# A hybrid decoder layer in fp32: even pauses in all eight mixer units, a later sample update in unit 0, products column tile by column tile, and ragged ends transposed together

## The chip, the cores and the metric

One core of one Trainium2 chip runs the whole program. The metric is the device time of one execution in microseconds (us), taken as the median of three runs. A profiled execution of the same program gives the trace from which the durations below are read; its own time stands beside its span in the table. TensorE is called PE here, VectorE DVE, ScalarE ACT, GpSimd POOL, and the queue of SyncE, which issues the DMAs, SP.

## The reference

One layer over 280 tokens: 16 learned meta tokens, 256 prompt tokens and 8 sample tokens, each sample with recurrent states of its own. The width is 2048; all is fp32.

```python
def decoder_layer(x, pos, s_ret, s_hg, prompt, ...):
    x = layer_norm(ALPHA * x + 0.5 * swiglu(x, f1_g, f1_u, f1_d), ln1_g, ln1_b)
    m, s_ret, s_hg = token_mixer(x, pos, s_ret, s_hg, prompt, w_in, lb, hg_norm_g, w_out)
    x = layer_norm(ALPHA * x + m, ln2_g, ln2_b)
    x = layer_norm(ALPHA * x + 0.5 * swiglu(x, f2_g, f2_u, f2_d), ln3_g, ln3_b)

def token_mixer(...):      # x @ w_in is split into ten parts of 2048 columns
    q_r, k_r, v_r, g_r, q_h, f_h, i_h, g_h, a_r, a_h = jnp.split(x @ w_in, N_PROJ, axis=-1)
    ...                    # retention: 8 heads of 256; HGRN2: 16 heads of 128, k = 1 - f
    y = jax.nn.sigmoid(a_r) * o_r + jax.nn.sigmoid(a_h) * o_h
    return y @ w_out, s_ret, s_hg

def retention_chunk(S, q, k, v):
    inner = jnp.einsum('bhid,bhjd->bhij', q, k) * D
    o = jnp.einsum('bhij,bhjv->bhiv', inner, v) + jnp.einsum('bhid,bhdv->bhiv', q_dec, S)
    S_new = jnp.exp(lg * C)[:, None, None] * S + jnp.einsum('bhjd,bhjv->bhdv', k_dec, v)
```

HGRN2 has the same form with a decay of its own for each feature and token. For each sample token both mixers read a state from memory, decay it, add one outer product of key and value, read the output from it with the query, and write it back. The two kinds of state of the 8 samples come to 8 MB for HGRN2 and 16 MB for retention, read once and written once.

## The kernel before

Features lie on the 128 partitions, tokens on the free axis: 280 columns, or 264 where the meta tokens are dropped. A weight of the width 2048 has 16 chunks of 128 features. Each fp32 weight product is made as three faster products (`dense()`, the matmul on L217): the weight's upper part by the input's upper part, the upper by the input's lower part (`xl`), and the weight's lower part (`wlo`) by the input's upper part. The weights stream in blocks of eight 128x128 tiles, 512 KB each (`stream()`): SP loads `raw`, ACT casts the upper part `whi` (L187), DVE subtracts for the lower part `wlo` (L188). There are three buffers of each, so a block is asked for some two blocks ahead of its use.

The program has three stages: the first feed-forward half-step (to about 742 us of the span), the mixer (to about 1790 us), and the output product with the second half-step. The change lies in the mixer alone. The mixer works in 8 units, each with one head of retention and two heads of HGRN2. For each unit `project()` makes six products of two chunks each (f, q_h, i_h, q_r, k_r, v_r), and then the four gate products of the unit before (g_r with a_r, g_h with a_h, twice). A step is one k-chunk of such a product: two weight tiles, six matmuls, about 0.7 us. A group has 16 steps, a unit 160.

Between the steps run the mixers' own small matmuls and transposes. Two generators for each unit, `mix_hg(u)` and `mix_ret(u)`, are started when their inputs are ready; each `yield n` is a pause of n steps, and after each step `pump()` counts the pauses down and lets a thread issue its next piece. So the order on PE is written out by hand, by these pauses. The order on ACT, DVE, POOL and SP is made by a scheduler that follows the program's priorities and its own estimates; there an instruction waits behind all that stands ahead of it on its engine.

In `mix_hg` the scores of a unit come level by level: `blocks()` makes the masked levels with 32-column tiles of PE (`pl`), later levels (16, 32, 64 tokens) use K and Q scaled on DVE, and a pause separates them. `calm` is an extra pause of two steps; it was left out in units 1 and 7 of `mix_hg` and in unit 7 of `mix_ret`, while unit 1 had two steps more at some places (`2 * (u == 1)`). Then K is transposed (`ptk`), the states of the samples are updated (`smh`, on ACT and DVE), and state, sample outputs and outputs are made (`pst`, `pq`, `po`, `pv`).

In `mix_ret` v and k are transposed, 128 tokens at a time (`pt`), cast and scaled (`vs`, `ks`), then come the scores (`psc`), the state (`psr`, copied by ACT to `sro`), and the samples' update: ACT scales the four loaded states by gamma (L1073, `smr<-smr,gam` for the first four samples and `smr<-smr,sro` for the last four), DVE adds the outer products (L1078), with each sample's value row spread over the partitions by a DMA (`vbr<-vrd`). Outputs (`pqr`, `por`, `pvr`) follow. The tokens do not divide by 128: 24 of k's and v's 280 columns and 16 of K's 272 are ragged ends, with a transpose of their own for each chunk or head.

Of the kernel before, what the change touches and what calls it, by code (L numbers as in the profile page):

```python
# [10 lines left out]
F32 = mybir.dt.float32  # L11
# [3 lines left out]
ALU = mybir.AluOpType  # L15
# [3 lines left out]
P = 128  # L19
# [31 lines left out]

SCORES = ((0, 0, SEQ, P), (SEQ, P - NMETA, 2 * P - P + NMETA, P), (2 * SEQ - P + NMETA, SEQ - NMETA, NMETA, LP - 2 * P))
# [75 lines left out]
def trunk(ctx: ExitStack, tc: tile.TileContext, A, O):  # L128
# [417 lines left out]
    with tc.tile_pool(name="yp", bufs=1) as yp:  # L546
# [7 lines left out]
        with tc.tile_pool(name="mp", bufs=1) as mp:  # L554
# [33 lines left out]
            qdh = tmp("qdh", (P, 2, NS * 32))  # L588
            qdr = tmp("qdr", (P, 2, NS * 32))
            nc.gpsimd.memset(qdh, 0.0)  # L590
            nc.gpsimd.memset(qdr, 0.0)
            vsm = tmp("vsm", (P, P))
# [8 lines left out]
            sc2 = tmp("sc2", (P, NMETA), dt=F32R)  # L601
            for z in (km, vm, ks2, vs2, sc2):
                z = z if len(z.shape) == 2 else z.rearrange("p c f -> p (c f)")
                nc.scalar.copy(z, qdh[:, 0, : z.shape[1]])
# [106 lines left out]
            def upper_upper_lower(out, x):  # L711
                n = x.shape[0]
                nc.scalar.copy(out[:n], x)
                nc.scalar.copy(out[32 : 32 + n], x)
                sub(out[64 : 64 + n], x, out[:n].bitcast(F32))
# [7 lines left out]
            def alone(qd, q):  # L723
                for e in range(2):
                    nc.vector.tensor_copy(qd[:, :, 128 * e + e : 128 * e + 128 : 32], q[:, :, SEQ + 4 * e : SEQ + 4 * e + 4])

            def sample_columns(on, po, os):

                nc.tensor.transpose(po[:, 3 * P :], os, ident)
                nc.vector.tensor_copy(  # L730
                    on[:, SEQ:].rearrange("p (e j) -> p e j", e=2), po[:, 3 * P :].rearrange("p (j c) -> p c j", c=32)[:, 0:2, :])

            def mix_hg(u, f, k, q, v):

                calm = 2 if u != 1 and u < HR - 1 else 0
# [62 lines left out]
                def blocks(x, s, own=None):  # L798

                    x = x.rearrange("p i (x j c) -> p i x j c", x=4, j=4)  # L800
                    for h in range(2):
                        pl = mx_bank("pl")
                        half = pl[:, : 2 * 80].rearrange("p (b c) -> p b c", b=2)
                        for b in range(2):
                            for j in range(0, P, 32):
                                kk = K[:, h, NMETA + b * P + j : NMETA + b * P + j + 32]
                                o = half[j : j + 32, b, :48].rearrange("p (i c) -> p i c", i=3)
                                nc.tensor.matmul(o, kk, x[:, :, 2 * h + b, j // 32, :], start=True, stop=True, tile_position=(0, j))
                                if own is not None:
                                    nc.tensor.matmul(  # L810
                                        half[j : j + 32, b, 48:], kk, own[:, h, b * P + j : b * P + j + 32],
                                        start=True, stop=True, tile_position=(0, j))
# [42 lines left out]
                for s in (4, 8):  # L855
                    scale_k(s)
                scale_q(8)
                join(8)
                yield W_LEVEL + 4 + 2 * (u == 1) + calm
                for s in LEVELS[MASKED:]:  # L860
# [29 lines left out]
                    yield W_LEVEL + 2 * (u == 1) + calm  # L890
# [6 lines left out]
                for h in range(2):  # L897
# [3 lines left out]
                    for b, (t0, n) in enumerate(((NMETA, P), (NMETA + P, P), (0, NMETA))):  # L901
                        nc.tensor.transpose(pt[:n, b * P : (b + 1) * P], K[:, h, t0 : t0 + n], ident)
                    nc.scalar.copy(kt, pt[:, : 2 * P].rearrange("p (b f) -> p b f", b=2))
                    upper_upper_lower(km[:, h, :], pt[:NMETA, 2 * P : 3 * P])
# [27 lines left out]
                for h in range(2):  # L932
                    for b in range(NS):
                        j = 32 * (b % 4)
                        nc.tensor.matmul(
                            pq[j : j + 32, h * P : (h + 1) * P], qdh[:, h, 32 * b : 32 * b + 32], sms[h][:, b, :],
                            start=b < 4, stop=b >= 4, tile_position=(0, j))
                os = tmp("osh", (P, 2 * P))
                nc.scalar.copy(os, pq[:, : 2 * P])
                yield 4  # L940

                def outputs(h):
# [5 lines left out]
                    sample_columns(on[:, h, :], po, os[:, h * P : (h + 1) * P])  # L948
# [31 lines left out]
            def mix_ret(u, q, k, v):  # L980
# [3 lines left out]
                calm = 2 if u < HR - 1 else 0  # L984
# [11 lines left out]
                nc.sync.dma_start(dt, A["dtab"][u])  # L996
                for c in range(2):
                    pt = mx_bank("pt")
                    for b, (t0, n) in enumerate(BLOCKS):
                        nc.tensor.transpose(pt[:n, b * P : (b + 1) * P], v[:, c, t0 : t0 + n], ident)  # L1000
                    nc.scalar.copy(vt[:, :, c, :], pt[:, : 2 * P].rearrange("p (b f) -> p b f", b=2))
                    nc.scalar.copy(vt2[:NB, c, :], pt[:NB, 2 * P : 3 * P])
                    f = slice(c * P, (c + 1) * P)
                    split(vs[:, 0, :, f], vs[:, 1, :, f], vt[:, :, c, :])
                    upper_lower_upper(vs2[:, c, :], vt2[:NB, c, :])
                    yield 1
                    pt = mx_bank("pt")
                    for b, (t0, n) in enumerate(BLOCKS):
                        nc.tensor.transpose(pt[:n, b * P : (b + 1) * P], k[:, c, t0 : t0 + n], ident)
                    for b, (t0, n) in enumerate(BLOCKS):  # L1010
                        x, g = pt[:n, b * P : (b + 1) * P], dec[:n, b, u : u + 1]
                        his = [ks[:, 0, b, f]] if b < 2 else [ks2[third[0], c, :], ks2[third[1], c, :]]
                        for hi in his:
                            nc.scalar.activation(hi, x, AF.Copy, scale=g)
                        nc.vector.scalar_tensor_tensor(
                            out=(ks[:, 1, b, f] if b < 2 else ks2[third[2], c, :]), in0=x, scalar=g,
                            in1=his[0].bitcast(F32), op0=ALU.mult, op1=ALU.subtract)
# [18 lines left out]
                gams = [tmp("gam", (P, 1))]  # L1036
                nc.gpsimd.tensor_scalar(
# [219 lines left out]
```

## Time and profile before

| what | value |
| --- | --- |
| median of 3 runs | 2599.12 us (2597.02 to 2599.78) |
| profiled execution, its own time | 2593.9 us |
| its span | 2592.1 us |
| PE busy | 2570.6 us, 99% of the span |
| DVE, ACT busy | 1703.8 us (66%), 1374.9 us (53%) |
| granted clock of PE | 0.999 |
| one steady unit (units 2 to 6) | 128.6 us |
| idle time of PE that ends on a wait | some 16 us in all |

A row of the timeline has the start in us from the span's start, the duration, the engine, the line, the operation, what is written and read by the program's names, and the number of such instructions; in square brackets stand the idle time of the engine just before it and what ended that. A matmul's shown duration is longer than the distance to the next, since they are pipelined: a cost on PE is read from the distance of starts. A row of the windows has, for each engine, its busy time in the stretch and the number of its instructions, then PE's granted clock, the share of time in which the DMA engines were busy, and GB/s.

### The profile page before, as it was taken

How to read it: one execution, taken by the hardware profiler on the slowest of the kernel's cores; microseconds unless marked ns; L12 is line 12 of the kernel's file. 1: busy time of each engine (PE TensorE's matmuls, PEld its weight loads, DVE VectorE, ACT ScalarE, POOL GpSimd, SP SyncE). 2: the span in 40 equal slices, each digit the busy share in tenths (PEclk: the TensorE clock that was granted, in tenths of full speed). 3: DMA queues.
4: the chain of work that ended last, by engine and by line, in shares of the span. 5: the costliest groups of instructions: out<-in, count | busy, mean ns of one | idle time of the engine just before them, and what ended most of it. 6: DMA issues, size and time to landing. Idle time of an engine off the chain costs nothing.

```text
span 2592.1 us, 56133 instructions
## 1 busy us (share of the span) xinstructions
PE 2570.6 (99%) x23400; PEld 2543.1 (98%) x23400; DVE 1703.8 (66%) x2859; ACT 1374.9 (53%) x2160; POOL 19.6 (1%) x78
## 2 busy tenths in 40 slices
PE   9999999999999999999999999999999999999999
PEld 9999999999999999999999999999999999999998
DVE  6544444565579787777787878786985555556555
ACT  5444444444456665757575757574564444444444
POOL 0000000000000000000000000000000000000000
PEclk9999999999999999999999999999999999999999
DMA  7555555555566786767676767666656666666664
GB/s 242 187 184 184 186 183 184 187 180 186 185 200 208 243 277 208 256 213 253 216 250 219 254 212 253 213 225 195 194 186 199 196 195 196 195 196 194 197 195 148
DMA packets 156895, 536.25 MB, mean 207 GB/s; under 512 B 17952, under 2 KB 25952, under 8 KB 156640
## 3 DMA queue, kind: packets, MB, share of 16 engines
q1 hardware_dynamic: 156352, 532.37, 63.2%
q8 instruction: 183, 3.00, 0.5%
q14 instruction: 72, 0.59, 0.1%
q10 hardware_dynamic: 288, 0.29, 0.0%
HBM read 501.99 MB, written 30.61 MB: 205 GB/s over the span
## 4 chain that ended last, share of the span: by engine, by line
PE 59%; DVE 1%; ACT 1%; issue 0%; POOL 0%; DVEq 0%; ACTq 0%; POOLq 0%
PE up L217 17%; PE dn L217 9%; PE wo L217 3%; PE pj_g_r L217 3%; PE pj_g_h L217 3%; PE pj_a_h L217 3%; PE pj_k_r L217 3%; PE pj_a_r L217 3%; PE pj_v_r L217 3%; PE pj_q_r L217 2%; PE pj_i_h L217 2%; PE pj_f L217 2%; PE pj_q_h L217 2%; DVE wlo L188 0%; PE pqr L1091 0%; PE por L1106 0%
## 5 line engine op out<-in xcount | busy, mean ns | idle before, releaser
L188 DVE TENSOR_TENSOR wlo<-raw,whi 128x1024 fp32r<-128x1024 f32 (+1 forms) x869 | 1062.8, 1223 | 762.1 <-ACT whi L187 760.5
L187 ACT CAST whi<-raw 128x1024 fp32r<-128x1024 f32 (+1 forms) x870 | 905.6, 1042 | 938.1 <-PE up L217 419.2
L217 PE MATMUL up<-xh,whi 128*128 128x280 f32 (+1 forms) x2624 | 725.6, 280 | 0.8 <-ACT whi L187 0.8
L217 PE MATMUL up<-xh,wlo 128*128 128x280 f32 (+1 forms) x2624 | 725.8, 280 | 0.4 <-DVE wlo L188 0.4
L217 PE MATMUL up<-xl,whi 128*128 128x280 f32 (+1 forms) x2624 | 725.4, 279 | 0.0
L217 PEld LDWEIGHTS up<-xh,whi 128*128 128x128 f32 x2624 | 492.6, 189 | 1.0 <-ACT whi L187 1.0
L217 PEld LDWEIGHTS up<-xh,wlo 128*128 128x128 f32 x2624 | 492.6, 189 | 1.0 <-DVE wlo L188 1.0
L217 PEld LDWEIGHTS up<-xl,whi 128*128 128x128 f32 x2624 | 492.6, 189 | 0.0
L217 PE MATMUL dn<-hh,whi 128*128 128x280 f32 (+1 forms) x1376 | 384.7, 280 | 0.0
L217 PE MATMUL dn<-hl,whi 128*128 128x280 f32 (+1 forms) x1376 | 384.3, 279 | 0.0
L217 PE MATMUL dn<-hh,wlo 128*128 128x280 f32 (+1 forms) x1376 | 384.3, 279 | 0.0
L217 PEld LDWEIGHTS dn<-hh,whi 128*128 128x128 f32 x1376 | 260.1, 189 | 0.1
L217 PEld LDWEIGHTS dn<-hl,whi 128*128 128x128 f32 x1376 | 260.1, 189 | 0.1
L217 PEld LDWEIGHTS dn<-hh,wlo 128*128 128x128 f32 x1376 | 260.1, 189 | 0.0
L217 PE MATMUL pj_g_r<-xh,whi 128*128 128x264 f32 x256 | 76.8, 300 | 0.0
L217 PE MATMUL pj_k_r<-xh,whi 128*128 128x280 f32 x256 | 73.7, 288 | 0.0
L217 PE MATMUL pj_g_h<-xh,whi 128*128 128x264 f32 x256 | 73.6, 288 | 0.0
L217 PE MATMUL pj_v_r<-xh,whi 128*128 128x280 f32 x256 | 73.5, 287 | 0.0
L217 PE MATMUL pj_v_r<-xh,wlo 128*128 128x280 f32 x256 | 72.4, 283 | 0.3 <-DVE wlo L188 0.3
L217 PE MATMUL pj_k_r<-xh,wlo 128*128 128x280 f32 x256 | 72.4, 283 | 0.0
L217 PE MATMUL pj_v_r<-xl,whi 128*128 128x280 f32 x256 | 72.3, 283 | 0.0
L217 PE MATMUL pj_k_r<-xl,whi 128*128 128x280 f32 x256 | 72.3, 283 | 0.0
(396 smaller groups left out, 5230.3 us busy)
## 6 DMA issues: line engine op xcount, KB each, us to landing
raw<-in_w_up SPq DMA_DIRECT2D x343, 512.0 KB
raw<-in_w_in SPq DMA_DIRECT2D x320, 512.0 KB
raw<-in_w_dn SPq DMA_DIRECT2D x172, 512.0 KB
smr<-in_sr SPq DMA_DIRECT2D x32, 512.0 KB
out_srs<-smr SPq DMA_DIRECT2D x32, 512.0 KB
raw<-in_w_out SPq DMA_DIRECT2D x32, 512.0 KB
smh<-in_sg SPq DMA_DIRECT2D x16, 512.0 KB
vbr<-vrd SPq DMA_DIRECT2D x32, 256.0 KB
```

Source lines behind the costliest of these rows:

```text
L187: nc.scalar.copy(hi[:, j:jn, :], raw[:, j:jn, :])
L188: nc.vector.tensor_tensor(out=lo[:, j0:j1, :], in0=raw[:, j0:j1, :], in1=hi[:, j0:j1, :].bitcast(F32), op=ALU.subtract)
L217: nc.tensor.matmul(o, w, t, start=start, stop=stop)
```

## The change

- `calm` is 2 in every unit of both mixers, and the special pauses of unit 1 are gone. Units 1 and 7 get the spacing of units 2 to 6.
- In unit 0 the pause behind the second state copy of retention is 10 steps rather than 2: the update of the samples' states, and the load of the last four samples' states (`load(1)`), come eight steps later.
- `blocks()` issues for each 128 tokens first the four 48-column products, one for each column tile, and then the four 32-column products, where before both products of a column tile stood next to each other.
- Ragged ends: POOL gathers the last 24 columns of both chunks of k and v in one tile (`tails`), which is transposed once in a unit rather than four times; POOL gathers the first 16 columns of both heads' K (`meta`), one transpose rather than two. The sample outputs of both HGRN2 heads are summed into one result of 128 columns (the queries are laid out with a row length of 129, `ALONE`, so that a head's queries take columns of their own), one copy and one transpose rather than a double-width copy and two transposes. The casts of v's ragged rows are made for both chunks at once and stand ahead of k's.
- `gam`, the tile with gamma, is made by POOL from the copy of the first half of retention's state, where before it was made from the scores. ACT's scaling of the first four samples therefore comes behind that copy. For the last four samples DVE takes the keys from a small copy that POOL makes (`late_k`).

```diff
-                calm = 2 if u != 1 and u < HR - 1 else 0          # mix_hg
+                calm = 2
...
-                            for j in range(0, P, 32):
-                                kk = K[:, h, NMETA + b * P + j : NMETA + b * P + j + 32]
-                                o = half[j : j + 32, b, :48].rearrange("p (i c) -> p i c", i=3)
-                                nc.tensor.matmul(o, kk, x[:, :, 2 * h + b, j // 32, :], start=True, stop=True, tile_position=(0, j))
-                                if own is not None:
+                            for mine in range(1 if own is None else 2):
+                                for j in range(0, P, 32):
+                                    at = b * P + j
+                                    o, y = half[j : j + 32, b, :48].rearrange("p (i c) -> p i c", i=3), x[:, :, 2 * h + b, j // 32, :]
+                                    if mine:
+                                        o, y = half[j : j + 32, b, 48:], own[:, h, at : at + 32]
                                     nc.tensor.matmul(
-                                        half[j : j + 32, b, 48:], kk, own[:, h, b * P + j : b * P + j + 32],
-                                        start=True, stop=True, tile_position=(0, j))
+                                        o, K[:, h, NMETA + at : NMETA + at + 32], y, start=True, stop=True, tile_position=(0, j))
...
+                nc.gpsimd.tensor_copy(meta[:, :, :NMETA], K[:, :, :NMETA])
...
-                yield W_LEVEL + 4 + 2 * (u == 1) + calm
+                yield W_LEVEL + 4 + calm
...
-                    yield W_LEVEL + 2 * (u == 1) + calm
+                    yield W_LEVEL + calm
...
-                    for b, (t0, n) in enumerate(((NMETA, P), (NMETA + P, P), (0, NMETA))):
-                        nc.tensor.transpose(pt[:n, b * P : (b + 1) * P], K[:, h, t0 : t0 + n], ident)
+                    for b in range(2):
+                        t0 = NMETA + b * P
+                        nc.tensor.transpose(pt[:, b * P : (b + 1) * P], K[:, h, t0 : t0 + P], ident)
+                    x = pt[:64, 2 * P : 3 * P]
+                    if h == 0:
+                        nc.tensor.transpose(x, meta.rearrange("p h t -> p (h t)"), ident)
...
-                calm = 2 if u < HR - 1 else 0                     # mix_ret
+                calm = 2
...
+                for i, x in enumerate((k, v)):
+                    nc.gpsimd.tensor_copy(tails[:, 2 * i : 2 * i + 2, :NB], x[:, :, 2 * P :])
                 for c in range(2):
                     pt = mx_bank("pt")
-                    for b, (t0, n) in enumerate(BLOCKS):
-                        nc.tensor.transpose(pt[:n, b * P : (b + 1) * P], v[:, c, t0 : t0 + n], ident)
+                    for b in range(2):
+                        nc.tensor.transpose(pt[:, b * P : (b + 1) * P], v[:, c, b * P : (b + 1) * P], ident)
...
-                    upper_lower_upper(vs2[:, c, :], vt2[:NB, c, :])
...
+                    if c == 0:
+                        nc.tensor.transpose(pt[:, 2 * P : 3 * P], tails.rearrange("p i t -> p (i t)"), ident)
+                    if c == 0:
+                        for i in range(2):
+                            r = 64 + 32 * i
+                            nc.scalar.copy(vt2[:NB, i, :], pt[r : r + NB, 2 * P : 3 * P])
+                        upper_lower_upper(vs2.rearrange("p c f -> p (c f)"), vt2.rearrange("p c f -> p (c f)")[:NB])
...
-                gams = [tmp("gam", (P, 1))]
-                nc.gpsimd.tensor_scalar(
-                    out=gams[0], in0=scr[:, 0:1], scalar1=GAMMA[u], scalar2=GAMMA[u], op0=ALU.min, op1=ALU.max)
...
-                    yield 2
+                    if c == 0:
+                        gams = [tmp("gam", (P, 1))]
+                        nc.gpsimd.tensor_scalar(
+                            out=gams[0], in0=so[:, 0:1], scalar1=GAMMA[u], scalar2=GAMMA[u], op0=ALU.min, op1=ALU.max)
+                    yield 2 if u or c == 0 else 10
                 load(1)
...
+                late_k = late[:, 1:].rearrange("p (c b) -> p c b", c=2)
+                nc.gpsimd.tensor_copy(late_k, k[:, :, LP + 4 :])
```

How the order moves, at three places. PE in unit 2, where the first chunk of v and k is transposed between the steps of a gate product, before:

```order
L1000 MATMUL pt<-ident,v 128x128 x2
L1000 MATMUL pt<-ident,v 24x128
L217 MATMUL pj_g_r_12858<-xh_3_9240,whi_12861 128x264
L217 MATMUL pj_g_r_12858<-xl_3_9241,whi_12861 128x264
L217 MATMUL pj_g_r_12858<-xh_3_9240,wlo_12862 128x264
L217 MATMUL pj_a_r_12859<-xh_3_9240,whi_12861 128x264
L217 MATMUL pj_a_r_12859<-xl_3_9241,whi_12861 128x264
L217 MATMUL pj_a_r_12859<-xh_3_9240,wlo_12862 128x264
L1009 MATMUL pt<-ident,k_r 128x128 x2
L1009 MATMUL pt<-ident,k_r 24x128
```

And the same place of PE now:

```order
L1022 MATMUL pt<-ident,v 128x128 x2
L218 MATMUL pj_g_r_12851<-xh_3_9247,whi_12854 128x264
L218 MATMUL pj_g_r_12851<-xl_3_9248,whi_12854 128x264
L218 MATMUL pj_g_r_12851<-xh_3_9247,wlo_12855 128x264
L218 MATMUL pj_a_r_12852<-xh_3_9247,whi_12854 128x264
L218 MATMUL pj_a_r_12852<-xl_3_9248,whi_12854 128x264
L218 MATMUL pj_a_r_12852<-xh_3_9247,wlo_12855 128x264
L1029 MATMUL pt<-ident,k_r 128x128 x2
L1031 MATMUL pt<-ident,tails 128x128
```

One transpose has gone from the first gap; the second has as many as before, and reads the new tile `tails`. In units 2 to 6 the gaps stand behind the same steps as before.

DVE in unit 0, around the retention samples' update (`smr<-vbr,k_r,smr`), between the lower parts of blocks 30 to 32 of the mixer's weights (`wlo30` to `wlo32`), before; `vbr_9960` holds the first value rows of the last four samples:

```order
L239 TENSOR_TENSOR K_9490<-K_9490,T4_9683 128x68x4
L254 TENSOR_TENSOR vs2_8641<-vt2_8636,vs2_8641 24x256
L239 TENSOR_TENSOR K_9490<-K_9490,T8_9892 128x34x8
L1078 SCALAR_TENSOR_TENSOR smr_9701<-vbr_9813,k_r_9445,smr_9701 128x256
L188 TENSOR_TENSOR wlo30_10032<-raw30_10030,whi30_10031 128x8x128
L1078 SCALAR_TENSOR_TENSOR smr_9703<-vbr_9813,k_r_9445,smr_9703 128x256 x2
L239 TENSOR_TENSOR T2_10876<-f_9916 128x272
L239 TENSOR_TENSOR T4_11042<-T2_10876 128x136
L239 TENSOR_TENSOR T8_11170<-T4_11042 128x68
L188 TENSOR_TENSOR wlo31_10091<-raw31_10089,whi31_10090 128x8x128
L1078 SCALAR_TENSOR_TENSOR smr_9937<-vbr_9960,k_r_9445,smr_9937 128x256
L188 TENSOR_TENSOR wlo32_10128<-raw32_10126,whi32_10127 128x8x128
```

And the same stretch of DVE now:

```order
L240 TENSOR_TENSOR K_9497<-K_9497,T8_9893 128x34x8
L1112 SCALAR_TENSOR_TENSOR smr_9707<-vbr_9810,k_r_9452,smr_9707 128x256
L189 TENSOR_TENSOR wlo30_9989<-raw30_9987,whi30_9988 128x8x128
L1112 SCALAR_TENSOR_TENSOR smr_9709<-vbr_9810,k_r_9452,smr_9709 128x256 x2
L1112 SCALAR_TENSOR_TENSOR smr_9707<-vbr_9812,k_r_9452,smr_9707 128x256 x2
L1112 SCALAR_TENSOR_TENSOR smr_9709<-vbr_9812,k_r_9452,smr_9709 128x256 x2
L189 TENSOR_TENSOR wlo31_10082<-raw31_10080,whi31_10081 128x8x128
L240 TENSOR_TENSOR T2_10875<-f_9918 128x272
L240 TENSOR_TENSOR T4_11053<-T2_10875 128x136
L240 TENSOR_TENSOR T8_11216<-T4_11053 128x68
L189 TENSOR_TENSOR wlo32_10131<-raw32_10129,whi32_10130 128x8x128
```

Six instructions of the update stood ahead of block 30's lower part before, two do now; six stand between blocks 30 and 31; and none on the last four samples stands ahead of block 32's any more. On SP the load of the second HGRN2 state (`smh`, 512 KB), which was issued behind the mixer's weight block 38, now stands between blocks 32 and 33, ahead of the two loads of the last four retention samples' states.

ACT in unit 2, between the last scaling of k and the second state copy, before:

```order
L880 COPY acch<-pl 64x2x64 x2
L1073 ACTIVATE smr<-smr,gam 128x1024
L187 CAST whi_13231<-raw_13230 128x8x128
L1073 ACTIVATE smr<-smr,gam 128x1024
L1058 COPY sro<-psr 128x256
L908 ACTIVATE smh<-smh,fs 128x128 x5
L1058 COPY sro<-psr 128x256
```

And now:

```order
L894 COPY acch<-pl 64x2x64 x2
L188 CAST whi_13219<-raw_13218 128x8x128
L927 ACTIVATE smh<-smh,fs 128x128 x3
L1084 COPY sro<-psr 128x256
L927 ACTIVATE smh<-smh,fs 128x128
L1106 ACTIVATE smr<-smr,gam 128x1024 x2
L1084 COPY sro<-psr 128x256
```

The two long scalings moved behind the first state copy, and the weight cast and three HGRN2 scalings moved ahead of them.

70 lines of the change are left out of this document (44 added, 26 removed).

## The prediction

> **What bounds the kernel.** I read the page's head first, then the stretch of one whole unit in the middle, then the rows of PE that carry a wait.
>
> ```profile
> span 2592.1 us, 56133 instructions
> PE 2570.6 (99%) x23400; PEld 2543.1 (98%) x23400; DVE 1703.8 (66%) x2859; ACT 1374.9 (53%) x2160; POOL 19.6 (1%) x78
> PEclk9999999999999999999999999999999999999999
> ```
>
> ```profile
> 1100.00:1228.60 128.60, 128.60 (x1274) 125.85 (x1273) 98.58 (x200) 82.45 (x156) 1.64 (x5) 1.00 0.71 235
> 1192.00:1200.00 8.00, 8.00 (x73) 7.90 (x72) 7.56 (x20) 7.96 (x18) 0.00 (x0) 1.00 0.95 330
> 836.00:844.00 8.00, 6.94 (x89) 6.58 (x88) 6.72 (x17) 5.05 (x6) 0.10 (x1) 1.00 0.90 310
> ```
>
> PE is the bound, at full clock: in a steady unit it is busy for all of 128.60 us, so a matmul taken away there shortens the span, as long as the weights keep up. The second row is the stretch in which they only just do (ACT busy 7.96 of 8 us). The third lies in unit 0, where PE does wait. The mixer's waits on PE:
>
> ```profile
> 840.01 0.38 PE L217 MATMUL pj_q_h<-xh,wlo 128*128 128x264 f32 x1 [1.06 <-DVE wlo L188]
> 847.51 0.39 PE L217 MATMUL pj_i_h<-xh,wlo 128*128 128x280 f32 x1 [1.31 <-DVE wlo L188]
> 852.09 0.41 PE L872 MATMUL pl<-Q,K 128*32 128x32 f32 x13 [2.40 <-DVE Q L239]
> 953.77 0.33 PE L902 MATMUL ptk<-ident,K 128*128 128x128 f32 x1 [1.45 <-DVE K L239]
> 969.09 0.30 PE L729 MATMUL por<-ident,osr 128*128 128x128 f32 x1 [1.75 <-ACT yh L224]
> 1692.16 0.33 PE L902 MATMUL ptk<-ident,K 128*128 128x128 f32 x1 [0.61 <-DVE km L254]
> 1701.72 0.38 PE L1056 MATMUL psr<-vs,ks 128*128 128x256 f32 x1 [1.48 <-DVE ks L1015]
> 1738.78 0.38 PE L236 MATMUL pvr<-rhi,ones_r 128*128 128x264 f32 x1 [0.37 <-ACT rhi L224]
> 1739.96 0.38 PE L236 MATMUL pvr<-rlo,ones_r 128*128 128x264 f32 x1 [0.81 <-DVE rlo L225]
> ```
>
> Three lie in unit 0 (4.77 us), two in unit 1 (3.20), four in unit 7 (3.27): just the units whose pauses are edited. Units 2 to 6 have none. So there are 11.2 us of waits to win, beside PE's own work.
>
> **Ragged ends.** Three transposes in a gap between dense products:
>
> ```profile
> 1172.52 0.28 PE L217 MATMUL pj_a_r<-xl,whi 128*128 128x264 f32 x1
> 1172.63 0.28 PE L217 MATMUL pj_a_r<-xh,wlo 128*128 128x264 f32 x1
> 1172.75 0.49 PE L1009 MATMUL pt<-ident,k_r 128*128 128x128 f32 x3
> 1172.99 0.36 PE L217 MATMUL pj_g_r<-xh,whi 128*128 128x264 f32 x1
> 1173.19 0.28 PE L217 MATMUL pj_g_r<-xl,whi 128*128 128x264 f32 x1
> ```
>
> A dense product starts 0.11 us after the one before it. From 1172.63 to 1173.19 pass 0.56 us, of which two dense products are 0.23; the three transposes cost 0.33, so 0.11 each. A unit loses five (two of v, one of k, one of K, one of the sample outputs; the first two and the next two become one and one): 40 x 0.11 = 4.4 us. The gathering copies on POOL are new, and this is how such copies run:
>
> ```profile
> 1134.22 0.97 POOL L737 COPY ends<-v 128x32 f32<-128x32 f32 x1 [75.17 <-ACT v L658]
> 1135.13 0.20 POOL L738 COPY ends<-v 128x32 f32<-128x32 f32 x1
> ```
>
> ```profile
> 1133.90 1.23 DVE L188 TENSOR_TENSOR wlo<-raw,whi 128x1024 fp32r<-128x1024 f32 x1 [1.42 <-ACT whi L187]
> ```
>
> ```profile
> 1170.28 0.40 ACT L675 COPY v<-pj_v_r 128x280 f32<-128x280 f32 x1
> ```
>
> The first copy took 0.97 us and ended at 1135.19, just behind the subtraction on DVE (1135.13); the next one took 0.20. In unit 2, v's second chunk is there at 1170.68 and the gap of k's first chunk is at 1172.75, 2.07 us later; a copy held behind a whole subtraction takes some 1.2 us, so the gathering of v lies hidden, with 0.9 us to spare, behind the gate products. I cost it at 0 (bounds: 0, and 1 us in each unit if one more subtraction comes between). `meta` is gathered over 20 steps before its use and has more cover. That POOL's reads hold up DVE I cost at 0 as well, since DVE is busy for 98.58 of 128.60 us in a unit; the bound is 4 reads x 8 units x 0.20 = 6.4 us. The copies that ACT and DVE save (two 24-row copies, two 24-row casts, the double-width sample copy) lie off the path and are worth nothing but slack.
>
> The Trainium skill (SBUF — State Buffer, "Who interferes with whom") says that a DVE instruction with two inputs in SBUF and a GpSimd instruction that reads SBUF take the same port by an exclusive lock, so that the second waits for the first to end. The copy above agrees (0.97 us behind the subtraction, 0.20 alone). By this rule each of the four added reads in a unit (two of `tails`, `meta`, the late keys) would also hold up DVE; if all of that fell on the path, the sum below would be -6.7 instead of -13.1.
>
> **Column tiles in turn.** The masked levels with and without the 32-column products:
>
> ```profile
> 1144.85 0.31 PE L808 MATMUL pl<-Qm,K 128*32 128x48 f32 x8
> 1145.69 0.39 PE L217 MATMUL pj_k_r<-xh,whi 128*128 128x280 f32 x1
> ...
> 1155.18 0.55 PE L808 MATMUL pl<-Qm,K 128*32 128x48 f32 x32
> 1155.66 0.39 PE L217 MATMUL pj_k_r<-xh,whi 128*128 128x280 f32 x1
> ```
>
> With them (64 products) the gap lasts 0.84 us, without (32) 0.48. So 32 products of 32 columns cost 0.36. The 32 of 48 columns, whose neighbours go to different column tiles, cost 0.48 less the 0.12 of a change-over, also 0.36. Taken in turn the narrower ones should cost 32/48 of that, 0.24: a gain of 0.12 in a unit, 1.0 us in eight. Bounds: 0 (the distance is set per instruction), and 8 x 0.36 = 2.9 (they vanish behind the others); I take 1.0, by the row of the same tiles.
>
> Against this speaks the Trainium skill (TensorE: Matmul & The Clock Gate, Part 3, "The mechanism"): a weight load overlaps running matmuls only where it goes to other rows of the array. All column tiles here use all 128 rows, so by that rule the order of the columns would change nothing, this term would be 0 and the sum -12.1. The cheap gap of 32 is as the column order lets one expect, but no row here has the other order with equal widths.
>
> **What of these 5.4 us is given back.** A steady unit has one tight place:
>
> ```profile
> 1325.48 0.28 PE L217 MATMUL pj_g_r<-xl,whi 128*128 128x264 f32 x1
> 1325.67 0.38 PE L217 MATMUL pj_g_r<-xh,wlo 128*128 128x264 f32 x1
> 1325.89 0.28 PE L217 MATMUL pj_a_r<-xh,whi 128*128 128x264 f32 x1
> ```
>
> Here a product comes 0.19 rather than 0.11 us after its neighbour, and the next 0.22 after it: the lower part was only just ready, behind ACT's fullest stretch (its like in unit 2 is the second windows row). PE will come there about 0.6 us earlier, while ACT has a few thin copies and casts less to do before it. I take 0.14 us a unit as given back in units 2 to 6, +0.7 us (bounds 0, and 5 x 0.68 = +3.4).
>
> **Pauses in units 1 and 7.** Unit 7 gets the spacing of units 2 to 6, which show no wait in any of their gaps: -3.27 us (bounds 0 and -3.27). Its last piece comes 18 steps later, still 10 steps ahead of the first gate product of unit 7 that could wait for it being done, so nothing is added at the end. In unit 1 the transposes of K come four steps (2.8 us) later, and the wait of 1.45 at 953.77 goes. The one at 969.09 stands behind a step that does not move, and waits for the sample outputs that DVE centres among many updates of HGRN2, which now come four steps later: I take half, -0.9 (bounds 0 and -1.75).
>
> **Unit 0's sample update, eight steps on.** DVE and ACT there:
>
> ```profile
> 834.71 1.27 DVE L1078 SCALAR_TENSOR_TENSOR smr<-vbr,k_r,smr 128x256 f32<-128x256 f32 x3
> ...
> 845.84 0.48 DVE L1078 SCALAR_TENSOR_TENSOR smr<-vbr,k_r,smr 128x256 f32<-128x256 f32 x1 [3.00 <-DMA vbr<-vrd]
> 846.24 1.22 DVE L188 TENSOR_TENSOR wlo<-raw,whi 128x1024 fp32r<-128x1024 f32 x1
> ...
> 851.62 0.42 DVE L239 TENSOR_TENSOR Q<-Q,T 128x256 f32<-128x256 f32 x1
> ```
>
> ```profile
> 840.72 1.15 ACT L1073 ACTIVATE smr<-smr,sro 128x1024 f32<-128x1024 f32 x1 [2.50 <-DMA smr<-in_sr]
> 842.29 1.15 ACT L1073 ACTIVATE smr<-smr,sro 128x1024 f32<-128x1024 f32 x1 [0.42 <-DMA smr<-in_sr]
> ```
>
> Four update instructions fewer stand ahead of block 30's lower part, 0.42 us each; but since they also wait less for their inputs I take only two of them as time saved, 0.85 of the wait of 1.06 at 840.01. The scaling of Q, which stood behind eight updates of the last four samples (from 845.84 on), now stands right behind block 32's lower part, some 3.5 us earlier: the 2.40 at 852.09 goes. Block 32 no longer waits behind DVE's 3.00 us for value rows. But its cast on ACT stands behind the scalings of the last four states, as before, and their loads now have 512 KB of HGRN2 state ahead of them: at 310 GB/s, 1.7 us. That brings the cast from 843.4 to some 845.1 and the lower part to 847.3, where it was 847.46 before. So the 1.31 at 847.51 stays, and I add 0.5 for a second thing late (bounds -1.3 and +3.0, the wait for value rows come back elsewhere). Unit 0: -0.85 - 2.40 + 0.5 = -2.75.
>
> **Gamma from the state's copy.** On ACT two scalings of 1.15 us move behind a state copy and one HGRN2 scaling, and the weight cast moves ahead of them. Between that copy and the scalings, POOL makes `gam`; the HGRN2 scaling covers part. I cost it at 0 (bounds: -0.2, since the cast is earlier, and +1.2 us in each unit where POOL is held behind a subtraction and ACT stands still).
>
> **The sum.** -4.4 - 1.0 + 0.7 - 3.3 - 1.45 - 0.9 - 2.75 = -13.1 us. The profiled execution took 2593.9 us, so it would take 2580.8; it lies 5.2 us under the median of 2599.12. The same difference from the median gives 2586.
>
> **Rivals.**
>
> 1. The work on PE goes and unit 7's waits go, but unit 0 and unit 1 only trade their waits: -5.4 + 0.7 - 3.3 = -8.0, so 2591. The same time comes out if the waits go but POOL's reads hold up DVE on the path by their 0.20 us each: -13.1 + 6.4 = -6.7, so 2592 (0.05 of this rival's chance). For it: 836 to 844 has DMA at 310 GB/s, and what is late there is a transfer. Against it: two of the waits are plain order on DVE.
> 2. The weights limit and most comes back: steady units return all of their 3.4 us, unit 0 waits 2 us more for the later states: -5.4 + 3.4 - 3.3 + 2.0 = -3.3, so 2596, within what can be told from no change (0.2%, 5.2 us). For it: ACT at 7.96 of 8 us. Against: ACT gets less to do.
> 3. Slower: the wait for `gam`. ACT now takes nothing behind it until state, copy and POOL are done, and the weight casts queue there. It decides when ACT loses more than (13.1 + 5.2) / 8 = 2.3 us in each unit ahead of the tight place; with one subtraction ahead of POOL (1.2 us) it does not. If the state copy itself is late by two steps (1.4 us) as well, that is 2.6 us, 8 x 2.6 = 20.8, and 2607. Against it: before, the copy followed the scalings without any idle time of ACT, and now a cast and three scalings stand ahead of it.
>
> **How the numbers follow.** The sum as worked out has a chance of 0.48, rival 1 0.26, rival 2 0.17, rival 3 0.09. The first two are faster by over 0.2%: 0.74; same 0.17; slower 0.09. The range goes down by the unknown bounds (columns 1.9 more, nothing returned 0.7, all waits of units 0 and 1 gone 2.9): -18.6, so 2580; and up to rival 2 with a microsecond for the spread of medians, 2597.
>
> **What would show it.** A steady unit of 128.0 us rather than 128.6; gaps of 0.72 rather than 0.84 us with the 32-column products; no wait of PE in unit 7; no wait for Q near 852 and one of about 1 us for the lower part near 847; ACT without idle time ahead of the scalings by `gam`. I am wrong if PE waits for a lower part near 1197, 1325 and their like in each unit by more than 0.5 us, if ACT shows waits for POOL, or if transposes of `tails` wait for POOL.

## The result, and the profile after

The changed kernel takes 2582.44 us in the median of six runs (2580.83 to 2583.04); the kernel before took 2598.1 us in six runs beside it (2597.02 to 2599.78). The ratio is 0.9939, with a 95% interval of 0.9927 to 0.9951: 15.7 us faster, where 13.1 were forecast. In a later comparison of the same two kernels the difference was 13.7 us. The profiled execution took 2582.39 us.

The head of the profile after, with its span, the busy time of the engines and PE's granted clock:

```profile
span 2580.6 us, 55997 instructions
PE 2565.8 (99%) x23360; PEld 2540.0 (98%) x23360; DVE 1702.4 (66%) x2827; ACT 1378.0 (53%) x2146; POOL 46.4 (2%) x112
PEclk9999999999999999999999999999999999999999
```

The six largest waits on PE, summed by line (in us: total, times, longest); those for `pw` and `up` lie in the feed-forward steps:

```profile
PE pl L881 <- DVE Q L240: 3.3, 1, 3.3
PE pw L515 <- DVE eps_h L163: 1.0, 1, 1.0
PE up L218 <- DVE wlo L189: 1.0, 3, 0.7
PE pj_i_h L218 <- DVE wlo L189: 0.8, 1, 0.8
PE pj_f L218 <- DVE wlo L189: 0.7, 1, 0.7
PE pj_i_h L218 <- ACT whi L188: 0.5, 1, 0.5
```

Of the nine mixer waits shown before, two have counterparts left (0.5 and 0.8, both near 846), and one is new: 3.3 us for Q, in unit 1. None of unit 7's is there. The 0.7 for `pj_f` is at 816.36; it and one of 0.31 at 803.37 were there before as well (0.88 at 815.90 and 0.31 at 802.76). Before there was also one of 0.47 at 1007.54 in unit 2, for POOL's `ends`, which is gone. The prediction's list did not have these three, so that units 2 to 6 showed no wait was not quite true.

The mixer's length can be read without the stages around it, from the first product of `f` to the first product of the last gate group. The timeline of PE before and then after, at these two starts:

```profile
745.13 0.28 PE L217 MATMUL pj_f<-xhg,whi 128*128 128x282 f32 x1
...
1777.98 0.28 PE L217 MATMUL pj_g_h<-xh,whi 128*128 128x264 f32 x1
```

```profile
745.75 0.28 PE L218 MATMUL pj_f<-xhg,whi 128*128 128x282 f32 x1
...
1766.42 0.28 PE L218 MATMUL pj_g_h<-xh,whi 128*128 128x264 f32 x1
```

1032.85 us became 1020.67, that is 12.18 less. (The mixer began 0.62 later, after a wait for weights in the first feed-forward step, which the change does not touch.) The starts of the products in between say where the time went. Unit 0's stretch, up to its first gate product, became 4.03 us shorter; unit 1's, up to the q_r product of unit 2, 0.37 longer; the rest of unit 2 0.65 shorter; the four units 3 to 6 together 2.98 shorter, which is 0.745 each on average (0.91, 0.40, 0.75 and 0.92); and unit 7, from its `f` on, 4.90 shorter.

Two gaps after, on PE: first the masked levels, then the transposes of v's first chunk. (They lie in unit 3, as do the rows from 1134 to 1201 that the prediction put into unit 2; the steady units are alike.)

```profile
1141.17 0.29 PE L824 MATMUL pl<-Qm,K 128*32 128x48 f32 x8
...
1141.92 0.39 PE L218 MATMUL pj_k_r<-xh,whi 128*128 128x280 f32 x1
```

```profile
1167.86 0.28 PE L218 MATMUL pj_a_r<-xh,wlo 128*128 128x264 f32 x1
1167.97 0.38 PE L1022 MATMUL pt<-ident,v 128*128 128x128 f32 x2
1168.11 0.36 PE L218 MATMUL pj_g_r<-xh,whi 128*128 128x264 f32 x1
1168.31 0.28 PE L218 MATMUL pj_g_r<-xl,whi 128*128 128x264 f32 x1
```

The first lasts 0.75 us instead of 0.84. In the second, 0.45 us pass from the last dense product ahead to the second one behind; two dense products are 0.23 of it and two transposes 0.22. So a transpose costs 0.11, as the sum had it.

The wait of 3.30 us for Q in unit 1 costs more than its idle time. Behind it PE's granted clock was 0.50 from 949.63 to 953.05, and dense products start 0.22 us apart instead of 0.11; that loses some 1.7 us more. Three windows of 3.2 us show this (PE's products are the first number in brackets, the clock is the third number from the end): the changed kernel behind that wait, then the kernel before behind unit 0's wait of 2.40 for Q, in the profile of before and in a second profile of the same kernel, where that wait was 2.40 again:

```profile
949.70:952.90 3.20, 3.20 (x17) 3.20 (x16) 1.38 (x5) 0.76 (x1) 0.20 (x1) 0.50 0.98 334
```

```profile
852.50:855.70 3.20, 3.20 (x30) 3.20 (x28) 3.17 (x8) 1.56 (x3) 0.00 (x0) 1.00 0.99 332
```

```profile
852.90:856.10 3.20, 3.20 (x17) 3.17 (x14) 2.84 (x8) 1.55 (x3) 0.00 (x0) 0.50 1.03 355
```

In the fourteen profiles of this case, all ten waits of 2.6 us or more in the mixer had such a stretch of 3.4 or 6.8 us, which began within the wait or at most 2.5 us behind it; of the two of 2.40 one had it, and of the seventeen from 1.0 to 1.8 us one.

### The profile page after: what moved, and what is told of

The parts are those of the page before. It is cut to its first block, busy times and chain, and to the rows that moved or that the text cites. A ratio compares the mean times of both kernels' runs of the same rounds, so it can differ in the third digit from the quotient of the medians.

```text
span 2580.6 us, 55997 instructions
## 1 busy us (share of the span) xinstructions
PE 2565.8 (99%) x23360; PEld 2540.0 (98%) x23360; DVE 1702.4 (66%) x2827; ACT 1378.0 (53%) x2146; POOL 46.4 (2%) x112
## 4 chain that ended last, share of the span: by engine, by line
PE 93%; DVE 3%; DMA 2%; ACT 1%; issue 1%; SPq 0%; DVEq 0%; ACTq 0%
PE up L218 34%; PE dn L218 19%; PE pj_v_r L218 4%; PE pj_i_h L218 3%; PE pj_g_r L218 3%; PE wo L218 3%; PE pj_q_r L218 3%; PE pj_f L218 3%; PE pj_k_r L218 3%; PE pj_a_r L218 3%; PE pj_g_h L218 3%; PE pj_a_h L218 3%; PE pj_q_h L218 3%; DVE wlo L189 1%; DMA raw<-in_w_up 1%
```

## The experiments

Each run is compared with the kernel before, run beside it. The mixer's length is read from each profile at the two starts named above. No run leaves work out.

| run | median, us | ratio to before (95%) | mixer in its profile, us |
| --- | --- | --- | --- |
| before, once more | 2596.32 | 1.0003 (0.9994 to 1.0012) | 1034.12 |
| changed, once more | 2581.56 | 0.9946 (0.9932 to 0.9960) | 1021.94 |
| changed, no pauses | 2591.26 | 0.9979 (0.9970 to 0.9987) | 1030.29 |
| before, only pauses | 2591.72 | 0.9982 (0.9973 to 0.9991) | 1027.72 |
| changed, products side by side | 2581.59 | 0.9946 (0.9933 to 0.9958) | 1020.51 |
| changed, unit 0 not later | 2587.58 | 0.9967 (0.9955 to 0.9980) | 1026.46 |
| changed, old unit 1 | 2580.94 | 0.9942 (0.9929 to 0.9954) | 1021.13 |
| changed, old unit 7 | 2587.98 | 0.9973 (0.9963 to 0.9983) | 1026.76 |
| changed, gamma from the scores | 2582.91 | 0.9948 (0.9934 to 0.9962) | 1024.26 |
| changed, unit 1 later too | 2575.84 | 0.9924 (0.9912 to 0.9936) | 1013.45 |
| the same, repeated | 2576.72 | 0.9929 (0.9915 to 0.9943) | 1015.14 |
| changed, all units later | 2576.68 | 0.9930 (0.9917 to 0.9943) | 1016.69 |

**The two kernels once more.** Nothing was edited.

> The kernel before once more, unchanged, with a profile of its own. The profile of before that was read took 2593.9 us, 4 us under the median of its six timed runs (2598.1). If that profile was a lucky execution, this one shows about 2598 and up to 4 us more waits of PE in units 0, 1 and 7 than the 11.2 us read before; if the profile was typical and the timed runs ran on a slower chip, this one shows about 2594 and the same waits. The ratio to the kernel before should be 1.000 within 0.001.

It came out between the two: 2596.8 us for the profiled execution, and the waits of units 0, 1 and 7 much as in the first profile. But in units 4 and 6 PE now waited for a lower part one weight block behind the tight rows that the prediction shows, where the first profile has no wait at all or 0.05 us:

```profile
1332.13 0.38 PE L217 MATMUL pj_g_r<-xh,wlo 128*128 128x264 f32 x1 [0.31 <-DVE wlo L188]
```

```profile
1589.92 0.38 PE L217 MATMUL pj_g_r<-xh,wlo 128*128 128x264 f32 x1 [0.61 <-DVE wlo L188]
```

In unit 0 the two waits for lower parts were 1.2 us shorter in all, but the clock was 0.50 for 3.4 us behind the wait for Q, as shown above. So the same program waits and slows down in some executions and not in others, and the profile that was read before was a favourable one: its mixer was 1.3 us shorter.

> The changed kernel once more, unchanged, beside the next runs on the same chip. Theory: PE's waits in the mixer are what the first profile showed (0.47 and 0.75 near 846, 3.30 at 948), and no wait in units 2 to 7; 13 to 16 us under the kernel before. Rival: the tight places of units 2 to 6 show waits in some executions as they do in the kernel before; then 0.3 us or more at 1195, 1325 or their like.

Measured: 13.7 us under the kernel before, and no wait in units 2 to 7 but 0.17 at 1072. Near 846 one wait of 0.57 stood instead of the two. The wait for Q in unit 1 varied, 5.04 us here against 3.30.

**The two halves alone.** The first of these two runs takes the pauses away from the changed kernel; the second puts them alone into the kernel before.

```diff
-                calm = 2                                   # mix_hg
+                calm = 2 if u != 1 and u < HR - 1 else 0
-                yield W_LEVEL + 4 + calm
+                yield W_LEVEL + 4 + 2 * (u == 1) + calm
...
-                calm = 2                                   # mix_ret
+                calm = 2 if u < HR - 1 else 0
...
-                    yield 2 if u or c == 0 else 10
+                    yield 2
```

> The changed kernel with all pauses as they were before (units 1 and 7, and unit 0's sample update). Theory: PE's own work is worth 40 x 0.11 + 8 x 0.09 = 5.1 us and the waits of units 0, 1 and 7 stay, so 5 us under the kernel before. Rival: the waits of units 0, 1 and 7 depend on the ragged ends too (fewer thin copies and casts on ACT and DVE), then 8 or more under it. Second rival: what PE saves returns as waits for weights, then 0 to 2 under it.

> The kernel before with the three edits of the pauses alone (two steps in every unit, unit 1's extra steps gone, unit 0's sample update eight steps later). Theory: the waits of unit 7 go (3.3 us), units 0 and 1 trade their 8.0 us for some 4.5, so 7 us under the kernel before; together with the run without pauses this adds up to the change. Rival: the pauses bring their gain only with the shorter ragged ends, then 3 us or less.

Without the pauses the gain over the kernel before is 4.8 us, about the theory's 5; with the pauses alone it is 4.4, less than the theory's 7 and more than the rival's 3. That sums to 9.2, and both together bring some 14; in the mixer 2.6 and 5.1 stand against 12.2. The two halves together bring more than the sum of what each brings alone. The waits on PE without the pauses show part of the reason:

```profile
PE pl L886 <- DVE Q L240: 3.9, 1, 3.9
PE ptk L917 <- ACT vtr L1023: 2.6, 1, 2.6
PE por L741 <- ACT yh L225: 1.8, 1, 1.8
PE ptk L917 <- DVE K L240: 1.1, 1, 1.1
```

The wait for Q in unit 0 has grown from 2.4 to 3.9, and in unit 7 K's transposes wait 2.6 us for ACT, where they waited 0.6; behind each of the two the clock was 0.50 for 3.4 us. In that profile a part of what PE saved (5.1 us) was given back there: the mixer is 2.6 us shorter than in the first profile of before, and 3.8 shorter than in the second. With the pauses alone, on the other hand, a new wait of 1.64 for ACT stands near 871 in unit 0, and this one behind the tight place of unit 3:

```profile
1199.83 0.38 PE L217 MATMUL pj_g_r<-xh,wlo 128*128 128x264 f32 x1 [1.09 <-DVE wlo L188]
```

**Column tiles.**

```diff
-                            for mine in range(1 if own is None else 2):
-                                for j in range(0, P, 32):
+                            for j in range(0, P, 32):
+                                for mine in range(1 if own is None else 2):
```

> The changed kernel with the two products of a column tile next to each other again, everything else as changed. Theory: the gap of the masked levels is 0.84 us again instead of 0.75, in eight units 0.7 us, so 0.7 us over the changed kernel. Rival (order of column tiles does not matter, the gap became shorter for another reason): the gap stays at 0.75 and the time is that of the changed kernel.

On PE the gap is 0.84 us again:

```profile
1141.02 0.31 PE L824 MATMUL pl<-Qm,K 128*32 128x48 f32 x8
...
1141.86 0.39 PE L218 MATMUL pj_k_r<-xh,whi 128*128 128x280 f32 x1
```

So the order of the columns is worth 0.09 us in a unit. The time does not show it: 2581.59 us lies between the changed kernel's two medians, 2582.44 and 2581.56, and eight times 0.09 is less than these differ. The steady units show it: units 3 to 6 take 127.75 to 127.76 us each in this run's profile, and 127.66 in the second profile of the changed kernel.

**Unit 0's sample update.**

```diff
-                    yield 2 if u or c == 0 else 10
+                    yield 2
```

> The changed kernel with unit 0's sample update eight steps earlier again (pause of 2 steps, as before), all else as changed. Theory: Q's scaling stands behind the updates of the last four samples again, and PE waits for Q near 852 by 2.4 to 3.9 us (3.9 in the run without any of the pauses); the kernel is 3 to 4 us over the changed one. Rival: what holds unit 0 is the weights' arrival, and the wait only stands at another place: within 1 us of the changed kernel.

It costs 5.1 to 6.0 us, and 5.8 in the mixer, more than the theory's 3 to 4. The wait is on PE, and it ends on DVE's scaling of Q, behind the eight updates of the last four samples and two subtractions:

```profile
851.41 0.33 PE L886 MATMUL pl<-Q,K 128*32 128x32 f32 x4 [3.96 <-DVE Q L240]
```

```profile
845.15 1.67 DVE L1112 SCALAR_TENSOR_TENSOR smr<-vbr,sro,smr 128x256 f32<-128x256 f32 x4
846.73 1.22 DVE L189 TENSOR_TENSOR wlo<-raw,whi 128x1024 fp32r<-128x1024 f32 x1
847.88 1.67 DVE L1112 SCALAR_TENSOR_TENSOR smr<-vbr,sro,smr 128x256 f32<-128x256 f32 x4
849.47 1.22 DVE L189 TENSOR_TENSOR wlo<-raw,whi 128x1024 fp32r<-128x1024 f32 x1
850.60 0.42 DVE L240 TENSOR_TENSOR K<-K,T 128x256 f32<-128x256 f32 x1
850.94 0.42 DVE L240 TENSOR_TENSOR Q<-Q,T 128x256 f32<-128x256 f32 x1
```

The same scaling in the changed kernel comes at 846.79, and PE does not wait. The theory had counted the idle time alone: behind this wait the clock was 0.50 until 856.49, which is some 2.3 us more (an estimate, half of the 4.6 us from 851.9 on).

**Unit 1, back and forth.** First the old spacing for unit 1 alone, then the later sample update for unit 1 as well as for unit 0.

```diff
-                calm = 2                                   # mix_hg
+                calm = 2 if u != 1 else 0
-                yield W_LEVEL + 4 + calm
+                yield W_LEVEL + 4 + 2 * (u == 1) + calm
```

> The changed kernel with the old spacing of unit 1 in the HGRN2 thread. Theory: the wait for Q (3.3) goes, and the two old waits of unit 1 (1.45 for K, 1.75 for the sample outputs) are back: within 1 us of the changed kernel, so that the edit of unit 1 is worth nothing. Rival: the old waits had their cause in the ragged ends and stay away: 3 us under the changed kernel.

Measured: 1.5 and 0.6 us under the changed kernel's two medians. The wait for Q is gone, and 0.98 for K and 1.75 for the sample outputs are back. The edit of unit 1 trades waits, and no gain of it can be told.

```diff
-                    yield 2 if u or c == 0 else 10
+                    yield 10 if u < 2 and c else 2
```

> The changed kernel with unit 1's sample update eight steps later too. Theory: the 3.3 us for Q at 948.40 have the cause that unit 0's 2.4 us had (Q's scaling behind updates of the last four samples, which wait for value rows), and go; 1.5 to 3.3 us under the changed kernel, less if the wait for the sample outputs (1.75 before) returns. Rival: the value rows are late because the DMA engines are full there, and a wait of 2 to 3 us stands at the next place: same time as the changed kernel.

> The run with unit 1's update eight steps later, repeated beside the changed kernel on the same chip. Theory: 6 to 7 us under the changed kernel, and no wait of PE over 0.8 us in the mixer. Rival: the first run of it was favoured by its chip or moment: then 3 us (the wait for Q alone) or less.

The first run was 6.6 us under the changed kernel's first median; beside the changed kernel on the same chip it was 4.8, and none of its five runs (2574.67 to 2579.62) lies among the other's five (2580.05 to 2583.21). Both gains are above the 3.3 us of the wait; the second lies between its theory (6 to 7) and its rival (3). In the changed kernel's timeline of DVE, Q's scaling stands behind updates that waited for their value rows:

```profile
943.54 0.42 DVE L240 TENSOR_TENSOR K<-K,T 128x256 f32<-128x256 f32 x1
945.10 0.48 DVE L1112 SCALAR_TENSOR_TENSOR smr<-vbr,sro,smr 128x256 f32<-128x256 f32 x1 [1.13 <-DMA vbr<-vrd]
945.50 1.22 DVE L189 TENSOR_TENSOR wlo<-raw,whi 128x1024 fp32r<-128x1024 f32 x1
946.64 1.27 DVE L1112 SCALAR_TENSOR_TENSOR smr<-vbr,sro,smr 128x256 f32<-128x256 f32 x3
947.83 0.42 DVE L240 TENSOR_TENSOR Q<-Q,T 128x256 f32<-128x256 f32 x1
```

With unit 1's update later, the two scalings stand ahead of these updates (second run):

```profile
942.29 0.42 DVE L240 TENSOR_TENSOR K<-K,T 128x256 f32<-128x256 f32 x1
942.63 0.42 DVE L240 TENSOR_TENSOR Q<-Q,T 128x256 f32<-128x256 f32 x1
942.96 0.87 DVE L1112 SCALAR_TENSOR_TENSOR smr<-vbr,sro,smr 128x256 f32<-128x256 f32 x2
```

and PE does not wait in unit 1. The stretch of unit 1 takes 93.11 us in the second run's profile instead of 98.15: some 3.4 of the 5.0 are the wait, and most of the rest is the clock, which stays at 1.00 in the mixer in both profiles of this version. This version is faster than both kernels.

> The changed kernel with the sample update eight steps later in all eight units, not in units 0 and 1 alone. Theory: the later update pays only where PE waits, and units 2 to 7 show no wait: as fast as with units 0 and 1 (about 2576) within 1.5 us. Rival: in the other units it pushes the update against the next state transposes and the weights: 3 us or more over that run.

```diff
-                    yield 2 if u or c == 0 else 10
+                    yield 10 if c else 2
```

Measured: 2576.68 us, the time of units 0 and 1 alone. In the other units there was nothing to win, and its profile shows waits at the tight places of units 2 and 6 (1.24 and 0.86) that the changed kernel's does not.

**Unit 7.**

```diff
-                calm = 2                                   # both threads
+                calm = 2 if u < HR - 1 else 0
```

> The changed kernel with unit 7's old spacing in both threads. Theory: unit 7's waits are back, and each costs its shown idle time and some 0.25 us more (the gaps of the profile of before were longer by that much than the idle time shown): 4 to 4.5 us over the changed kernel, where the prediction put 3.3. Rival: with the shorter ragged ends unit 7's waits are mostly gone anyway: less than 2 us over it.

It costs 6.4 us against the changed kernel beside it, and 5.6 us in the mixer from unit 7's `f` on, more than the theory's 4 to 4.5. The waits are not those of before, but two others:

```profile
PE ptk L917 <- ACT vtr L1023: 2.7, 1, 2.7
PE psc L1056 <- ACT kth L923: 0.9, 1, 0.9
```

ACT's casts of v's ragged rows and the scaling of the HGRN2 states now stand ahead of its copy of v, and PE waits for that copy. Behind these two waits the clock was 0.50 from 1689.18 to 1692.60.

**Gamma's place.** The tile is made from the scores again, as in the kernel before.

> The changed kernel with gamma made from the scores again, so that the scaling of the first four samples' states need not follow the first state copy. Theory: ACT's order goes back, with one scaling ahead of a weight cast; the lower part is late at the tight place of units 2 to 6 by 0.1 to 0.6 us as in the second profile of before (0.31 and 0.61 at 1332 and 1590), and the kernel is 0.5 to 2.5 us over the changed one. Rival: the tight place was relieved by the fewer thin copies and casts alone: no wait of PE in units 2 to 6 and the time of the changed kernel.

The median is 0.5 and 1.4 us over the changed kernel's two. In the profile the mixer is 3.6 us longer: in unit 0 three waits for weights' lower parts (1.37, 0.77, 1.03) and one of 0.47 for the sample outputs, in unit 1 a wait for Q of 4.02, and 0.34 behind the tight place of unit 3, which is 1.0 us longer. So that wait did come back, in one of the steady units; 2.9 us lie in unit 0, where the theory had nothing.

## Why the forecast came out as it did

**PE's own work: right.** A transpose costs 0.11 us and 40 are gone, 4.4 us. The masked levels gained 0.09 us in a unit, not 0.12: 0.7 us in all instead of 1.0. From the Trainium skill (TensorE: Matmul & The Clock Gate, Part 3, "The mechanism"), by which a weight load overlaps running matmuls only where it goes to other rows, I had worked out that the order of the columns would change nothing. That did not come out here: the gap is 0.84 us with one order and 0.75 with the other, with nothing else changed. What makes the difference is not shown.

**What is given back: wrong in sign, but for unit 2.** I put +0.14 us in each steady unit. In units 3 to 6 a unit became 0.745 us shorter on average, which is PE's own 0.64 and 0.1 more, since the tight place eased as well:

```profile
1320.72 0.28 PE L218 MATMUL pj_g_r<-xl,whi 128*128 128x264 f32 x1
1320.84 0.34 PE L218 MATMUL pj_g_r<-xh,wlo 128*128 128x264 f32 x1
1321.01 0.28 PE L218 MATMUL pj_a_r<-xh,whi 128*128 128x264 f32 x1
```

0.12 and 0.17 us, where it was 0.19 and 0.22. In unit 2 it went the other way: a wait of 0.17 stands at 1071.61, and the second group of g_r with a_r is 0.44 us longer than before. Of the 0.65 us that the rest of unit 2 lost, 0.44 is the wait for POOL's `ends`, which no term of the sum had. What the change is worth there does not all show against the first profile of before, since that execution hardly waited. In nine profiles that have both the shorter ragged ends and gamma's new place, and the sample update late in units 0 and 1 at most, no wait over 0.18 us stands at or behind the tight places; in the second profile of before, with the pauses alone, and with gamma from the scores, there are waits of 0.31 and 0.61, 1.09, and 0.34. That both edits are needed for it is likely from these runs, not shown: each was left out in one or two profiles, and the thing varies from execution to execution.

**Unit 7: right in cause, too small.** I took the four idle times, 3.27. From unit 7's `f` on 4.90 went, some 0.64 of it PE's own work. One reason can be read from the gaps: a wait costs more than the idle time shown with it. The gap of `psr` that waited 1.48 was 1.74 longer than its like, and that of `ptk` which waited 0.61, 0.83 longer, because the idle time begins only at the modelled end of the last matmul. The pauses are worth more still within the changed kernel (5.6 to 6.4 us), since the shorter ends alone bring other waits there, with the clock at 0.50 behind them.

**Unit 0: right in cause, too small.** The wait for Q went as described. The states behind the extra 512 KB were there at 842.03 instead of 840.72, but the mixer began 0.62 later; in the second profile of the changed kernel, where it began at 745.13 as before, they were there at 840.78. So the lateness of 1.7 in the estimate is not confirmed. The waits near 846 are 1.22, in that second profile 0.57, where I had 1.31 and 0.5 more. Of the 4.03 us that unit 0 lost, 0.64 is PE's own work and 3.4 are waits, where I had 2.75. In executions like the second profile of before, the stretch at 0.50 behind the wait for Q goes with it. What I had not seen is that gamma's new place delays the first update in unit 0. ACT waits there for POOL:

```profile
832.76 2.19 ACT L1106 ACTIVATE smr<-smr,gam 128x1024 f32<-128x1024 f32 x2 [1.29 <-POOL gam L1088]
```

and the first update on DVE starts at 833.94 instead of 832.78 (0.62 of this is the mixer's later start). That PE loses by it is not shown: with gamma from the scores unit 0 took 2.9 us more, not less.

**Unit 1: the step that failed.** I put -1.45 for the wait for K and -0.9 for half of that for the sample outputs. Both waits did go, but unit 1 became 0.37 us longer, in spite of 0.64 us of PE's work saved, because a new wait of 3.30 for Q stands at 948.40, with the clock at 0.50 behind it. It is the mechanism that I had described for unit 0: a scaling of Q behind updates that wait for value rows. I had read where PE's pieces go in unit 1 and not where DVE's go. And the sum counted every wait at its idle time; that a long one also slows the products behind it, here by 1.7 us, was in no term. The first rival said that units 0 and 1 only trade their waits; for unit 1 that is what happened, for unit 0 not. Without unit 1's trade the change would have gained some 5 to 6.5 us more, as the version with unit 1's update later shows.

**Gamma's wait: small.** ACT waits 0.22 to 0.23 us for POOL in units 3 to 7, 0.15 in unit 2, 0.58 in unit 1 and 1.29 in unit 0. I had named waits of ACT for POOL as a sign of being wrong; they came, but the third rival needed 2.3 us in every unit. POOL's copies run as the row of `ends` let one expect, 0.9 to 1.1 us behind a subtraction, and no transpose waits for them. DVE's subtractions of lower parts take 1.22 us on average in the mixer before and after (1.23 at most after), so POOL's added reads did not lengthen these.

**The sum.** Read by the mixer, -13.1 stands against -12.2: unit 1 fell 3.4 us short of its part of the forecast (-3.03), and unit 0 (by 0.6), the steady units (by 0.9) and unit 7 (by 0.95) went beyond theirs. That the total came so near is in part luck, since these misses nearly cancel. The medians moved by more than the profiles, 13.7 to 15.7 against 11.5; the likely reason is that the profile of before was a favourable execution.

## What to carry to other kernels

When the hand-written order of one engine moves, read the new order of the engines that feed it at every place that moves, not only where a wait stood: here a wait of 3.2 us in unit 1 was traded for one of 3.3, by a queue order that the same page explained for unit 0. A long wait of PE is to be counted with what follows it: here 3.3 us of idle time came with 1.7 us more at half the clock. Two edits whose waits end in the same queue don't add up, so each is best measured by taking it out of the finished version. And a profile is one execution: where a stage runs with 0.05 us to spare, a second profile of the same kernel says what it costs as a rule.

## What the runs showed that I had not expected

The same program waits at the tight places in one execution and not in the next (0 and 0.31 us at the same place in unit 4 of the kernel before; 3.30 and 5.04 for Q in unit 1 of the changed one), and behind the same wait of 2.40 us the clock fell to 0.50 in one and not in the other. And PE's savings of 5.1 us, taken without the pauses, showed as only 2.6 to 3.8 us in the mixer of that profile, while the waits for Q in unit 0 and for ACT in unit 7 grew.
